# A hybrid decoder layer on one core: in the attention's blocks on TensorE the scores move ahead of the transposes, and two pairs' values move together

## The chip, the cores and the metric

The kernel runs on 1 core of one Trainium2 chip. The metric is device time in microseconds (us), the median of several runs. One further execution was taken by the hardware profiler; all rows of the trace are of that one.

Engines: PE is TensorE (matmuls), PEld its weight loads, DVE is VectorE, ACT is ScalarE, POOL is GpSimd, SP issues the DMAs.

## The reference, cut to what matters

One decoder layer, 256 tokens, width 1024, 8 heads of 64. With 256 tokens there is one MoBA block of 256 keys, so the attention is causal within it.

```
h = rmsnorm(x, norm_mix_g)
q, k, v, u_pool, gate_logits = split(h @ w_in)
q = rotary(rmsnorm(q, q_norm_g)); k = rotary(rmsnorm(k, k_norm_g))
attn = softmax(causal(q @ k.T * 64**-0.5)) @ v
pooled = multiscale_pool_mixer(u_pool, w_pool, pool_scale)
gates = sigmoid(gate_logits + b_gate)
x = x + (gates[0] * (attn @ w_branch_attn) + gates[1] * (pooled @ w_branch_pool)) @ w_out
h2 = rmsnorm(x, norm_ffn_g)
gate, val = split(causal_depthwise_conv(h2 @ w_up, conv_w, conv_b))
out = x + (silu(gate) * val) @ w_down
```

## The kernel before, in words

**Weights.** Each weight arrives by DMA as chunks of 128 x 2048 float32 (`raw`) and is split into a high part (`hi`, ACT, line 87) and a low part (`lo`, DVE, line 91), both of type float32r. A product is then three matmuls: high by high, low by high, high by low (`mm3`, lines 99 to 101). `ahead()` records the next splits between the matmuls of the current work, and a freed `raw` buffer starts the next load.

**Stages.** q, k and v (line 298), the pool inputs `u`, sixteen gate tiles `g0` to `g15` (24 matmuls each, `feature_tile`), eight tiles of the pool branch `bp` (12 matmuls each, `branch`), eight of the attention branch `ba`, the output projection, and the FFN (`up`, `down`), which fills the second half of the time.

**The attention** is put between the gate tiles and the pool branch's tiles, by pairs of heads `hp` = 0 to 3, in plain float32. For each pair there are three pieces on PE:

- `scores(hp)`: q by k, 4 matmul calls (lines 473, 474). Both heads have a contraction of 64, so one stands on rows 0 to 63 of the array and the other on rows 64 to 127 (the trace prints the array's part as 64\*128). Then DVE adds the mask and takes the maxima, ACT takes the exponentials, POOL multiplies by the reciprocal sums.
- `weigh(hp)`: six transposes of the probabilities, 128x128 each (line 506, tile `ps_p`, whole array, 128\*128); ACT copies the result to `pT` (line 508).
- `values(hp)`: v by `pT`, 4 matmul calls (line 517, tile `ps_o`). The two heads write 64 partitions each, so the trace prints 128\*64. ACT and DVE then make `ath` and `atl`, which the attention branch reads.

A matmul call in float32 is two instructions in the trace, a transpose is one; so the scores and the values have 8 each, the transposes 6.

**The order.** All is recorded in program order and every engine runs its own instructions in that order. `later(n, fn)` files a piece for n ticks later; `tick()` comes after every gate tile, and in the pool branch after the odd tiles. `scores` stands ahead of g1, g5, g9 and g13; `weigh` is filed 4 ticks after its scores, so it comes just after g4, g8, g12 and after `bp1`; `values` another 4 ticks later (after g8, g12, bp1), for the last pair 1 tick (after `bp3`). So between two gate tiles there stand together: after g4 the transposes of pair 0 and the scores of pair 1; after g8 the values of pair 0, the transposes of pair 1, the scores of pair 2; after g12 the same one pair on; after bp1 the values of pair 2 and the transposes of pair 3; after bp3 the values of pair 3.

**PSUM.** Pool `ps2` has two buffers of two banks each (scores, transposes and the pool maps `ps_m` use it in turn), pool `mm` four of one bank (all tiles, and the values).

Of the kernel before, what the change touches and what calls it, by code (L numbers as in the profile page):

```python
# [8 lines left out]
F32 = mybir.dt.float32  # L9
# [5 lines left out]
P = 128  # L15
# [7 lines left out]
KA = AW // P  # L23
# [43 lines left out]
def hybrid_layer_kernel(ctx: ExitStack, tc: tile.TileContext, xq_d, xtok_d, par_d, wkv_d, wpg_d,  # L67
# [11 lines left out]
    ps2 = pairs.enter_context(tc.tile_pool(name="ps2", bufs=2, space=bass.MemoryType.PSUM))  # L79
    tmp = mixer.enter_context(tc.tile_pool(name="tmp", bufs=2))  # L80

    def bank(name):
        return mm.tile([P, 512], F32, tag="mm", name=name)


    def high(hi, src, scale=1.0):
        nc.scalar.activation(hi, src, AF.Copy, scale=scale)  # L87

    def low(lo, hi, src, scale=None):
        if scale is None:  # L90
            nc.vector.tensor_tensor(lo, src, hi.bitcast(F32), ALU.subtract)  # L91
        else:
            nc.vector.scalar_tensor_tensor(lo, src, scale, hi.bitcast(F32), ALU.mult, ALU.subtract)
# [59 lines left out]
    def next_high():  # L153
        if at[0] < len(pieces):
            c, sl, first, _ = pieces[at[0]]
            if c - oldest() >= WBUFS:
                return
            at[0] += 1
            if first:
                moving = order[c][0] in "qkv"  # L160
                place = MOVING if moving else 0
                his[c] = whi_p.tile([P, CH + P], F32R, tag="whi", name=f"hi_{order[c][0]}{c}")[:, place:]
                place = MOVING if moving else FAR
                los[c] = wlo_p.tile([P, CH + P], F32R, tag="wlo", name=f"lo_{order[c][0]}{c}")[:, place:]
            high(his[c][:, sl], raw(c, sl))

    def next_low(eager=False):
        if at[1] < at[0] - STAGGER or at[0] == len(pieces) > at[1] or (at[1] < at[0] and eager):
            c, sl, _, last = pieces[at[1]]
            at[1] += 1  # L170
            low(los[c][:, sl], his[c][:, sl], raw(c, sl))
            if last:
                split.add(c)
                while loaded[0] - RAWBUFS in split and order[loaded[0] - RAWBUFS][0] != "q" and loaded[0] < len(order):
                    load()
# [221 lines left out]
    def later(n, fn, *args):  # L397
        due.setdefault(clock[0] + n, []).append((fn, args))
# [67 lines left out]

    TOK = (slice(0, P), slice(P, 3 * P))

    def scores(hp):
        ps = ps2.tile([P, 2, 512], F32, tag="ps2", name=f"ps_s{hp}")  # L470
        for j in range(2):
            rows = slice(j * DH, (j + 1) * DH)
            nc.tensor.matmul(ps[:, j, P:3 * P], qT[rows, hp, P:S], kT[rows, hp, :], start=True, stop=True)
            nc.tensor.matmul(ps[:, j, 0:P], qT[rows, hp, 0:P], kT[rows, hp, 0:P], start=True, stop=True)
        if hp == 0:

            for _ in range(2):
                next_high()
        sm = tmp.tile([P, 2, 3 * P], F32, tag="big", bufs=4, name=f"sm{hp}")
        nc.vector.tensor_tensor(sm, ps[:, :, 0:3 * P],  # L480
                                mask.rearrange("p a b -> p (a b)")[:, None, :].to_broadcast([P, 2, 3 * P]), ALU.add)
        mx = tmp.tile([P, 2, 2], F32, tag="mx", name=f"mx{hp}")
        for t in (1, 0):
            nc.vector.tensor_reduce(mx[:, t, :], sm[:, :, TOK[t]], axis=AX.X, op=ALU.max)
        nc.vector.scalar_tensor_tensor(mx, mx, -1.0, qs[:, :, 2 * hp:2 * hp + 2], ALU.mult, ALU.mult)
        if hp == 0:
            for _ in range(2):
                next_low()
        sums = tmp.tile([P, 2, 2], F32, tag="sums", name=f"sums{hp}")
        for j in range(2):  # L490
            for t in (1, 0):
                nc.scalar.activation(sm[:, j, TOK[t]], sm[:, j, TOK[t]], AF.Exp, bias=mx[:, t, j:j + 1],
                                     scale=qs[:, t, 2 * hp + j:2 * hp + j + 1], accum_out=sums[:, t, j:j + 1])
        rs = tmp.tile([P, 2, 2], F32, tag="rs", name=f"rs{hp}")
        nc.vector.reciprocal(rs, sums)
        for t in (1, 0):
            n = TOK[t].stop - TOK[t].start
            nc.gpsimd.tensor_tensor(sm[:, :, TOK[t]], sm[:, :, TOK[t]],
                                    rs[:, t, :, None].to_broadcast([P, 2, n]), ALU.mult)
        later(4, weigh, hp, sm)  # L500

    def weigh(hp, sm):
        pp = ps2.tile([P, 2, 512], F32, tag="ps2", name=f"ps_p{hp}")
        for j in range(2):
            for b in range(3):
                nc.tensor.transpose(pp[:, j, b * P:(b + 1) * P], sm[:, j, b * P:(b + 1) * P], ident)
        pT = tmp.tile([P, 2, 3 * P], F32, tag="big", bufs=4, name=f"pT{hp}")
        nc.scalar.activation(pT, pp[:, :, 0:3 * P], AF.Copy)
        later(1 if hp == KA - 1 else 4, values, hp, pT)

    def values(hp, pT):

        po = bank(f"ps_o{hp}")
        for b in range(2):
            for j in range(2):
                h = 2 * hp + j
                nc.tensor.matmul(po[j * DH:(j + 1) * DH, b * P:S], vn[:, b, h * DH:(h + 1) * DH],
                                 pT[:, j, 2 * b * P:(2 * b + 2 - b) * P], start=b == 0, stop=b == 1)
        high(ath[:, hp, :], po[:, 0:S])
        low(atl[:, hp, :], ath[:, hp, :], po[:, 0:S])  # L520
# [26 lines left out]
    for n in range(2 * KD):  # L547
        if n >= FIRST and (n - FIRST) % 4 == 0:
            scores((n - FIRST) // 4)
        if n == 10:  # L550
            pool_maps()
            ahead()
        b, c = n // 2, n % 2
        if c == 0:
            w = chunk("g")
        ps = feature_tile(w, c, f"g{n}")
        tick()
        ahead(AHEAD if n % 2 else 0)
        nc.vector.tensor_tensor(gate(n), ps[:, 0:S], R1, ALU.mult)
        if n >= 2 * KD - 2:  # L560
            sigmoids(3)
# [213 lines left out]
    last = {}  # L775
# [71 lines left out]
```

## Time and profile before

| what | value |
|---|---|
| median of 3 runs | 335.42 us (335.11 to 335.70) |
| the profiled execution's own time | 335.33 us |
| its span, first to last instruction | 333.6 us |
| PE busy / weight loads busy | 328.6 us (99%) / 319.5 us (96%) |
| DVE / ACT / POOL busy | 254.9 (76%) / 202.6 (61%) / 82.3 us (25%) |
| granted TensorE clock, mean | 0.998 |

The span lies 1.73 us below the execution's own time. "Busy" of PE counts an instruction from its start to its modelled end, so two matmuls that overlap in the pipeline look like one, and a matmul that waits for its weights inside its own row still looks busy. What PE loses is better seen in the time from one matmul to the next.

### The profile page before, as it was taken

What the parts mean: (1) busy time and instruction counts of PE and PEld (TensorE: products, weight loads), DVE (VectorE), ACT (ScalarE), POOL (GpSimd) and SP (SyncE); (2) the same over time, 40 slices, a digit from 0 to 9 for tenths busy, and PEclk for the clock granted to TensorE, in tenths of its full rate; (3) what the DMA queues carried; (4) which work ended last, traced back from release to release, by engine and by line L of the source; (5) the groups of instructions that cost most, each with busy time, mean ns of one, the idle gap of its engine ahead of it and who ended that gap; (6) DMA issues with size and microseconds to landing.
All of it is one profiled execution on the core that took longest, in us unless ns stands there. A gap on an engine that the chain in (4) does not pass through costs nothing.

```text
span 333.6 us, 6696 instructions
## 1 busy us (share of the span) xinstructions
PE 328.6 (99%) x2728; PEld 319.5 (96%) x2728; DVE 254.9 (76%) x408; ACT 202.6 (61%) x326; POOL 82.3 (25%) x98
## 2 busy tenths in 40 slices
PE   8999999999999999999999999999999999999995
PEld 7888899999999999999999999999999999999995
DVE  4939979979778866877997977777777777768844
ACT  5767626645849945767766766555656464646520
POOL 1007771102404034121241212121212121221330
PEclk9999999999999999999999999999999999999999
DMA  7999763474455660763529283636454555543003
GB/s 266 422 415 205 226 271 129 157 253 149 145 210 181 218 235 2 252 210 110 209 106 358 72 328 129 252 130 252 140 240 146 233 163 216 182 198 128 0 2 126
DMA packets 11102, 63.94 MB, mean 192 GB/s; under 512 B 1472, under 2 KB 2752, under 8 KB 4032
## 3 DMA queue, kind: packets, MB, share of 16 engines
q1 hardware_dynamic: 10656, 63.39, 53.3%
q8 instruction: 21, 0.34, 0.4%
q10 hardware_dynamic: 416, 0.13, 0.3%
q14 instruction: 9, 0.07, 0.1%
HBM read 62.47 MB, written 1.05 MB: 190 GB/s over the span
## 4 chain that ended last, share of the span: by engine, by line
PE 97%; DMA 1%; ACT 0%; DVE 0%; issue 0%
PE ps_up L99 12%; PE ps_up L101 12%; PE ps_up L100 12%; PE ps_d L707 6%; PE ps_d L709 6%; PE ps_d L708 6%; PE ps_g L99 5%; PE ps_g L101 4%; PE ps_g L100 4%; PE ps_q L298 3%; PE ps_k L298 3%; PE ps_v L298 3%; PE ps_out L99 2%; PE ps_out L101 2%; PE ps_out L100 2%; DMA xq<-in_xq 1%
## 5 line engine op out<-in xcount | busy, mean ns | idle before, releaser
L101 PE MATMUL ps_up<-hhi,lo_up 128*128 128x256 f32 x352 | 97.2, 276 | 0.0
L99 PE MATMUL ps_up<-hhi,hi_up 128*128 128x256 f32 x352 | 97.2, 276 | 0.0
L100 PE MATMUL ps_up<-hlo,hi_up 128*128 128x256 f32 x352 | 97.2, 276 | 0.0
L100 PEld LDWEIGHTS ps_up<-hlo,hi_up 128*128 128x128 f32 x352 | 66.1, 188 | 0.0
L101 PEld LDWEIGHTS ps_up<-hhi,lo_up 128*128 128x128 f32 x352 | 66.1, 188 | 0.0
L99 PEld LDWEIGHTS ps_up<-hhi,hi_up 128*128 128x128 f32 x352 | 66.1, 188 | 0.0
L91 DVE TENSOR_TENSOR lo_up<-raw_up,hi_up 128x1024 fp32r<-128x1024 f32 x44 | 54.7, 1261 | 7.3 <-ACT hi_up L87 7.3
L707 PE MATMUL ps_d<-ah,hi_dn 128*128 128x256 f32 x176 | 48.6, 276 | 0.0
L708 PE MATMUL ps_d<-al,hi_dn 128*128 128x256 f32 x176 | 48.6, 276 | 0.0
L709 PE MATMUL ps_d<-ah,lo_dn 128*128 128x256 f32 x176 | 48.6, 276 | 0.0
L689 POOL TENSOR_TENSOR c_v<-c_g,c_v 128x256 f32<-128x256 f32 x22 | 16.2, 736 | 121.4 <-DVE c_v L672 121.4
L87 ACT ACTIVATE hi_up<-raw_up 128x1024 fp32r<-128x1024 f32 x44 | 44.1, 1047 | 0.0
L87 ACT ACTIVATE ah<-c_v 128x256 fp32r<-128x256 f32 x22 | 9.2, 418 | 45.6 <-POOL c_v L689 45.6
L99 PE MATMUL ps_g<-xhi,hi_g 128*128 128x256 f32 x128 | 35.9, 280 | 0.0
L100 PE MATMUL ps_g<-xlo,hi_g 128*128 128x256 f32 x128 | 35.3, 276 | 0.0
L101 PE MATMUL ps_g<-xhi,lo_g 128*128 128x256 f32 x128 | 35.3, 276 | 0.0
L707 PEld LDWEIGHTS ps_d<-ah,hi_dn 128*128 128x128 f32 x176 | 33.0, 188 | 0.0
L708 PEld LDWEIGHTS ps_d<-al,hi_dn 128*128 128x128 f32 x176 | 33.0, 188 | 0.0
L709 PEld LDWEIGHTS ps_d<-ah,lo_dn 128*128 128x128 f32 x176 | 33.0, 188 | 0.0
L91 DVE TENSOR_TENSOR lo_dn<-raw_dn,hi_dn 128x1024 fp32r<-128x1024 f32 x22 | 27.8, 1263 | 0.4 <-ACT hi_dn L87 0.4
L677 DVE TENSOR_TENSOR u_v<-ps_up,R 128x256 f32<-128x256 f32 x22 | 9.3, 421 | 20.9 <-PE ps_up L101 20.8
L714 POOL TENSOR_TENSOR al<-c_v,ah 128x256 fp32r<-128x256 f32 x22 | 22.0, 1002 | 11.6 <-ACT ah L87 11.6
(188 smaller groups left out, 794.7 us busy)
## 6 DMA issues: line engine op xcount, KB each, us to landing
raw_up<-in_wup SPq DMA_DIRECT2D x22, 1024.0 KB, 4.9
raw_dn<-in_wdn SPq DMA_DIRECT2D x11, 1024.0 KB, 4.9
raw_g<-in_wpg SPq DMA_DIRECT2D x8, 1024.0 KB, 5.9
raw_o<-in_wout SPq DMA_DIRECT2D x4, 1024.0 KB, 4.7
raw_v<-in_wkv SPq DMA_DIRECT2D x2, 1024.0 KB, 15.4
raw_p<-in_wpg SPq DMA_DIRECT2D x2, 1024.0 KB, 12.9
raw_bp<-in_wbp SPq DMA_DIRECT2D x2, 1024.0 KB, 4.8
raw_ba<-in_wba SPq DMA_DIRECT2D x2, 1024.0 KB, 4.7
```

The costliest lines, as they stand in the source:

```text
L87: nc.scalar.activation(hi, src, AF.Copy, scale=scale)
L91: nc.vector.tensor_tensor(lo, src, hi.bitcast(F32), ALU.subtract)
L99: nc.tensor.matmul(out, sh, mh, start=start, stop=False, **kw)
L100: nc.tensor.matmul(out, sh, ml, start=False, stop=False, **kw)
L101: nc.tensor.matmul(out, sl, mh, start=False, stop=stop, **kw)
L298: nc.tensor.matmul(pt[t], sx[:, k, t * P:(t + 1) * P], wx[:, sl], start=k == 0 and sx is xhi and wx is hi, stop=k == KD - 1 and wx is lo)
L677: nc.vector.tensor_tensor(u, ps[:, 0:S], R2, ALU.mult)
L689: nc.gpsimd.tensor_tensor(uc[1], g[1], uc[1], ALU.mult)
L707: nc.tensor.matmul(o, hi[:, sl], acch[i], start=first, stop=False, skip_group_check=True)
L708: nc.tensor.matmul(o, hi[:, sl], accl[i], start=False, stop=False, skip_group_check=True)
L709: nc.tensor.matmul(o, lo[:, sl], acch[i], start=False, stop=i == KF - 1, skip_group_check=True)
L714: nc.gpsimd.tensor_tensor(accl[i], act_i, acch[i].bitcast(F32), ALU.subtract)
```

## The change

`weigh` of pairs 0 to 2 no longer runs at its tick. It is put on a list (`held`), and the next `scores` runs it right after its own matmuls. `weigh` of pair 3 runs at its tick as before. `values` of pair 2 is filed 5 ticks after its `weigh` in place of 4, which is the tick of pair 3's values; these two write the two banks of one `ps2` buffer (`ps_oo`) in place of two `mm` buffers.

```
+    held = []
+
     def scores(hp):
         ps = ps2.tile([P, 2, 512], F32, tag="ps2", name=f"ps_s{hp}")
         for j in range(2):
             rows = slice(j * DH, (j + 1) * DH)
             nc.tensor.matmul(ps[:, j, P:3 * P], qT[rows, hp, P:S], kT[rows, hp, :], start=True, stop=True)
             nc.tensor.matmul(ps[:, j, 0:P], qT[rows, hp, 0:P], kT[rows, hp, 0:P], start=True, stop=True)
+
+        while held:
+            weigh(*held.pop())
...
-        later(4, weigh, hp, sm)
+        later(4, weigh if hp == KA - 1 else lambda *a: held.append(a), hp, sm)
...
-        later(1 if hp == KA - 1 else 4, values, hp, pT)
+
+        later((4, 4, 5, 1)[hp], values, hp, pT)
+
+    last = []
 
     def values(hp, pT):
 
-        po = bank(f"ps_o{hp}")
+        if hp < KA - 2:
+            po = bank(f"ps_o{hp}")
+        elif hp == KA - 2:
+            last.append(ps2.tile([P, 2, 512], F32, tag="ps2", name="ps_oo"))
+            po = last[0][:, 0, :]
+        else:
+            po = last[0][:, 1, :]
```

How the order on the engines changes, at three places (names as built, with buffer numbers; the shapes are the outputs').

PE between gate tiles g12 and g13: values of pair 1 (`ps_o`), transposes of pair 2 (`ps_p`), scores of pair 3 (`ps_s`). Before:

```order
L517 MATMUL ps_o_1145<-pT_976,vn 64x256 x2
L517 MATMUL ps_o_1145<-pT_976,vn 64x128 x2
L506 MATMUL ps_p_1152<-ident,sm_990 128x128 x6
L473 MATMUL ps_s_1164<-qkT 128x256
L474 MATMUL ps_s_1164<-qkT 128x128
L473 MATMUL ps_s_1164<-qkT 128x256
L474 MATMUL ps_s_1164<-qkT 128x128
```

The same place now:

```order
L531 MATMUL ps_o_1145<-pT_988,vn 64x256 x2
L531 MATMUL ps_o_1145<-pT_988,vn 64x128 x2
L475 MATMUL ps_s_1155<-qkT 128x256
L476 MATMUL ps_s_1155<-qkT 128x128
L475 MATMUL ps_s_1155<-qkT 128x256
L476 MATMUL ps_s_1155<-qkT 128x128
L511 MATMUL ps_p_1160<-ident,sm_990 128x128 x6
```

The transposes moved from between values and scores to behind the scores, next to g13. The place after g8 reads the same; after g4 there are no values, and transposes and scores change places.

PE in the pool branch, after bp1 and after bp3 (the 12 matmuls of each `bp` tile are left out here). Now, behind bp1 and then behind bp3:

```order
L511 MATMUL ps_p_1312<-ident,sm_1169 128x128 x6
L531 MATMUL ps_oo<-pT_1167,vn 64x256 x2
L531 MATMUL ps_oo<-pT_1167,vn 64x128 x2
L531 MATMUL ps_oo<-pT_1319,vn 64x256 x2
L531 MATMUL ps_oo<-pT_1319,vn 64x128 x2
```

The first row stands alone behind bp1, where the values of pair 2 stood ahead of it; the other four stand behind bp3, where the values of pair 3 stood alone.

ACT over the same two tiles (`pT`: the copy of the transposes of pair 3; `ath`: the high part of the values; `hi_ba`: a weight split; the `xq` rows are sigmoids). Before:

```order
L527 ACTIVATE xq<-xq,par 128x256
L87 ACTIVATE ath<-ps_o_1312 128x256
L508 ACTIVATE pT_1326<-ps_p_1319 128x768
L87 ACTIVATE hi_ba_1328<-raw_ba_1117 128x1024
L527 ACTIVATE xq<-xq,par 128x256
L87 ACTIVATE hi_ba_1328<-raw_ba_1117 128x1024
L527 ACTIVATE xq<-xq,par 128x256
L87 ACTIVATE ath<-ps_o_1366 128x256
```

Now:

```order
L541 ACTIVATE xq<-xq,par 128x256
L513 ACTIVATE pT_1319<-ps_p_1312 128x768
L87 ACTIVATE hi_ba_1321<-raw_ba_1117 128x1024
L541 ACTIVATE xq<-xq,par 128x256
L87 ACTIVATE hi_ba_1321<-raw_ba_1117 128x1024
L541 ACTIVATE xq<-xq,par 128x256
L87 ACTIVATE ath<-ps_oo 128x256 x2
```

The `ath` of pair 2 left its place ahead of the copy and stands beside that of pair 3. On DVE its low part moved likewise; nothing else changes there. In the gate tiles the copy `pT` moves behind one weight split on ACT, still ahead of the exponentials.

## Rows read from the trace of the kernel before

**Rows 1.** The page's busy line, and the waits of PE (us in total, times, longest).

```profile
PE 328.6 (99%) x2728; PEld 319.5 (96%) x2728; DVE 254.9 (76%) x408; ACT 202.6 (61%) x326; POOL 82.3 (25%) x98
...
PE ps_warm L228 <- DVE ones L196: 1.1, 1, 1.1
PE ps_q L298 <- ACT hi_q L87: 0.4, 1, 0.4
```

**Rows 2.** Windows: stretch, length, busy PE PEld DVE ACT POOL, PEclk, DMA, GB/s.

```profile
78.09:80.99 2.90, 2.90 (x27) 2.14 (x26) 2.39 (x4) 1.36 (x3) 0.00 (x0) 1.00 0.89 302
...
110.89:112.11 1.22, 1.22 (x12) 0.78 (x11) 1.22 (x2) 1.22 (x3) 0.00 (x0) 1.00 0.41 54
112.11:117.45 5.34, 5.34 (x48) 5.34 (x48) 4.46 (x9) 4.99 (x11) 0.00 (x0) 1.00 0.77 267
```

**Rows 3.** Chain that ended last, between g0 and g1: start us, us, what.

```profile
53.80 0.64 PE ps_s L473 x4
54.44 0.22 PE ps_s L474 x4
54.66 0.31 PE ps_g L99
```

**Rows 4.** The same chain between g4 and g5.

```profile
65.74 0.66 PE ps_p L506 x6
66.39 0.64 PE ps_s L473 x4
67.03 0.22 PE ps_s L474 x4
67.25 0.32 PE ps_g L99
```

**Rows 5.** The same chain between g8 and g9.

```profile
78.37 0.80 PE ps_o L517 x8
79.17 0.81 PE ps_p L506 x6
79.97 0.64 PE ps_s L473 x4
80.61 0.22 PE ps_s L474 x4
80.84 0.31 PE ps_g L99
```

**Rows 6.** The same chain between g12 and g13, first and last piece.

```profile
93.28 0.80 PE ps_o L517 x8
...
95.74 0.31 PE ps_g L99
```

**Rows 7.** The same chain behind bp1.

```profile
106.82 0.80 PE ps_o L517 x8
107.62 0.81 PE ps_p L506 x6
108.43 0.12 PE ps_bp L99
```

**Rows 8.** The same chain behind bp3.

```profile
111.16 0.80 PE ps_o L517 x8
111.96 0.32 PE ps_bp L99
```

**Rows 9.** Timeline of PEld at g0's end and g4's end: start, us, instruction.

```profile
53.72 0.31 PEld L473 LDWEIGHTS ps_s<-qkT 64*128 64x128 f32 x4
...
65.48 0.67 PEld L506 LDWEIGHTS ps_p<-ident,sm 128*128 128x128 f32 x6
```

**Rows 10.** Timelines of DVE, PE and ACT at the buffers that change hands.

```profile
81.44 0.95 DVE L480 TENSOR_TENSOR sm<-ps_s,mask 128x768 f32<-128x768 f32 x1
...
83.59 0.28 PE L99 MATMUL ps_m<-poolh,hi_pool 128*128 128x256 f32 x1
...
109.06 0.79 ACT L508 ACTIVATE pT<-ps_p 128x768 f32<-128x768 f32 x1
```

## Prediction

> **What bounds the kernel now.** I read the busy line and the waits first. PE is busy 328.6 of 333.6 us, and its waits for other engines are two at the very start, 1.1 and 0.4 us [rows 1]. So from the first projection on nothing holds PE back but PE: every engine behind it has room, and the time is the sum of what stands on PE. Next I read the windows, to see whether the attention's pieces cost clock: across the whole block after g8 the granted clock is 1.00, the 2.4 GHz level, and it is the same in the pool branch [rows 2]. A change in the order of PE's instructions can then act in two ways only: through what PE loses between its instructions, or through a new wait for another engine.
>
> What it loses is seen in the chain that ended last, which there is PE's own sequence. The reader should compare the length of one kind of piece after different neighbours. The six transposes take 0.66 us behind a gate tile [rows 4] and 0.81 us behind values [rows 5, 7]. The first matmul of a tile takes 0.31 or 0.32 us behind scores and behind values [rows 3, 4, 5, 8], but 0.12 us behind transposes [rows 7]. The scores take 0.64 + 0.22 = 0.86 us behind a gate tile and behind transposes alike [rows 3, 4, 5]. The values, always behind a tile, take 0.80 us [rows 5, 6, 7, 8]. So there is a charge at some borders and none at others. It is 0.81 - 0.66 = 0.15 us for entering transposes and 0.31 - 0.12 = 0.19 us (0.20 with 0.32) for entering a tile, and it falls where the part of the array changes: scores use 64\*128, tiles and transposes 128\*128 [rows 9], values 128\*64. Between tiles and transposes the part stays the same, and there is no charge in either direction. The weight loads show why: ahead of transposes the first load stands at 65.48, 0.26 us before the 65.74 at which the chain begins that piece, while ahead of scores it stands at 53.72, only 0.08 us before 53.80 [rows 3, 4, 9]. At a border of this kind the load isn't drawn ahead under the matmuls in front of it.
>
> The Trainium skill (TensorEngine Tiling (Array Packing), Key Properties) says that changing the tiling mode, not just the tile, drains TensorE. The charges above are that drain, at 0.15 to 0.20 us each; the page gives no price, and the sum below goes by the rows.
>
> **The change, part by part.** I call a border that changes the part a switch.
>
> *After g4.* Before: transposes 0.66, scores 0.86, first matmul of g5 0.32, which is 1.84 us [rows 4]. Now scores come behind a tile, 0.86 as after g0 [rows 3]; transposes come behind scores; the first matmul of g5 comes behind transposes, 0.12 [rows 7]. Transposes behind scores have no row. Behind a part that doesn't change they take 0.66, behind values 0.81. I take 0.81, since scores change the part as values do. Sum 1.79, so -0.05 us. Two switches stand there before and after; only their prices differ. With 0.66 it would be -0.20.
>
> *After g8 and g12.* Before: 0.80 + 0.81 + 0.86 + 0.31 = 2.78 us [rows 5], and the second place has the same length, 93.28 to 95.74 against 78.37 to 80.84 [rows 5, 6]. There are four switches: into values, into transposes, into scores, into the tile. Now it is values 0.80, scores behind values, transposes behind scores 0.81, tile 0.12: three switches. Scores behind values have no row either. From below they take 0.86 less a switch, some 0.67; from above the 0.86 that they take behind whatever the rows show. I take 0.86, as both their neighbours in the rows are a change of part and values to scores is one too (128\*64 to 64\*128). Sum 2.59, so -0.19 at each place, -0.38 for both.
>
> *Behind bp1.* Before: values 0.80, transposes 0.81, tile 0.12, which is 1.73 [rows 7]. Now the transposes alone, with tiles on both sides: 0.66 + 0.12 = 0.78 [rows 4, 7]. That is -0.95.
>
> *Behind bp3.* Before: 0.80 + 0.32 [rows 8]. Now two pairs' values in a row, and the second needs no switch. Values without a switch have no row: at most 0.80, and at least 0.80 less the dearest entry, 0.20, which is 0.60. I take 0.65, the 0.80 less the 0.15 that the transposes pay for entering behind values, the nearest row. That is +0.65, with ends at +0.60 and +0.80. Behind bp1 and bp3 together: -0.30, two switches fewer.
>
> *Other engines.* ACT, DVE and POOL do what they did, so nothing is removed there. ACT's copy `pT` moves behind one weight split in the gate tiles, and stays ahead of exponentials that can't start before DVE has the maxima; values need it only four ticks later. No DMA is added or moved in SP's queue.
>
> *Buffers.* The turn of the two `ps2` buffers changes. The pool maps, ahead of g10, now get the buffer of pair 2's scores, which is free when DVE has added the mask: 81.44 + 0.95 = 82.39. PE reaches the maps at 83.59, or 83.35 with the 0.24 us saved by then [rows 10]. That leaves 0.96 us, and before it was a transposes' copy long done, so no cost as long as DVE keeps its time. The values of pair 3 need the copy of pair 3's transposes, done at 109.06 + 0.79 = 109.85 before [rows 10]. ACT is full there (1.22 of 1.22 us behind bp3, 4.99 of the next 5.34 [rows 2]), so I let the copy gain only the `ath` row that leaves its front, and bound its end by 109.85 above and some 0.3 us less below, about 109.55. The values of pair 2 now begin 0.05 + 0.38 + 0.95 = 1.38 us earlier than 111.16, at 109.78, and those of pair 3 0.65 later, at 110.43. That leaves 0.6 to 0.9 us: again no wait. What both feed, the attention branch, starts at 117.45 [rows 2] behind four more tiles.
>
> **Sum.** -0.05 - 0.38 - 0.95 + 0.65 = -0.73 us. PE waits for nothing behind it, so all of it should reach the end. Against the profiled execution, 335.33 us, this gives 334.60; its span would be 332.9. That execution lies 0.09 below the median of the runs, 335.42, so the median should be **334.69 us**, 0.22% less. A measurement of this kernel can tell about 0.2%, 0.67 us, from no change; the forecast lies 0.06 us beyond that bound, so its own chances are split there.
>
> **The rivals.**
>
> *1. Scores behind values are free, and transposes behind scores too.* If the charge hung on the kind of work and not on the part (float32 pieces with half-array shapes as one kind), values to scores would cost nothing: another 0.19 at each of two places, -1.11 in all, 334.3 us; with transposes at 0.66 too, 0.15 more at each of three places. For it: no row shows the two side by side. Against it: every row where the part changes shows a charge. The page's rule on tiling modes speaks against it too, since 128 by 64 and 64 by 128 are different modes there. Chance 0.10.
>
> *2. Part of it is given back in small change.* The first matmuls behind a switch sometimes follow each other at 0.12 in place of 0.11 us; the second pair's values may pay the whole 0.80. With that 0.15 and some 0.15 of such small change the sum is -0.43, 334.99 us, which counts as the same. Chance 0.14.
>
> *3. A new wait behind bp3, slower than before.* ACT is full there and PE now arrives 1.38 us earlier, with 0.6 to 0.9 us to spare for the copy of pair 3's transposes. From the point at which that copy comes more than 0.9 us late PE waits, and what stands behind on PE waits with it. It eats the whole gain when the copy is 0.9 + 0.73 = 1.63 us late, and makes the kernel slower by more than 0.67 from 2.3 us on, two weight splits or three. With 2.4 us it gives 335.42 - 0.73 + 1.5 = 336.2 us. For it: ACT's full windows. Against it: the order puts no split ahead of the copy that wasn't there before, and one `ath` fewer. Chance 0.04.
>
> *4. The change does nothing that counts.* The charges in the chain would be an artefact of where the profile puts a matmul's end, and the order of pieces would be free: 335.4 us. Against it: the same pieces agree at all places to 0.01 us, and the windows in front and behind add up. Chance 0.05.
>
> **How the numbers follow.** The forecast has 0.67; measured with some 0.25 us of spread (the three runs lie within 0.6 us), 0.06 us beyond the bound, it gives 0.38 faster and 0.29 same. Rival 1 gives 0.10 faster, rivals 2 and 4 0.19 same, rival 3 0.04 slower. Together 0.48 faster, 0.48 same, 0.04 slower. The range reaches from rival 1, 334.3 less 0.1 of spread, up to rival 2 with its spread, 335.2: **334.2 to 335.2 us**.
>
> **What the profile after would show.** Right: in the chain after g8 and g12 values 0.80, scores 0.86, transposes 0.81, tile 0.12; behind bp1 transposes 0.66; behind bp3 sixteen instructions of values in about 1.45 us, then a tile's first matmul at 0.32; PE's waits still only those at the start; a span near 332.9 us. Scores behind values shorter than 0.75 us would show rival 1. A wait of PE for ACT's `pT` in the pool branch would show rival 3, and one for DVE's `sm` ahead of the pool maps its like. The forecast is wrong if the pieces shorten as said and the span doesn't: then something behind, DVE or a weight's arrival, was closer to PE than its missing waits tell.

## The result and the profile after

The change made the kernel slower: 338.62 us (median of six runs, 337.34 to 338.82) against 335.34 us before (335.11 to 335.70), a ratio of 1.0088 (95% interval 1.0070 to 1.0106). The forecast was 334.69 us with a range up to 335.2. The profiled execution took 338.81 us, 3.48 more than that of before, on a span of 337.0 us.

First the line and the view with which the prediction began: the page's busy line of the changed kernel, and the waits of PE (total us, times, longest).

```profile
PE 329.9 (98%) x2728; PEld 320.9 (95%) x2728; DVE 255.6 (76%) x408; ACT 202.8 (60%) x326; POOL 82.4 (24%) x98
...
PE ps_oo L531 <- DVE atl L91: 2.2, 1, 2.2
PE ps_warm L228 <- DVE ones L196: 1.1, 1, 1.1
PE ps_q L298 <- ACT hi_q L87: 0.3, 1, 0.3
```

Against [rows 1] there is one wait more, and it is the only one past the first microseconds: PE waited 2.2 us for DVE's `atl` before it could write `ps_oo`, the buffer that the values of pairs 2 and 3 share. Now the windows (columns as in [rows 2]), from the end of bp3 to the start of the attention branch:

```profile
109.69:113.80 4.11, 1.92 (x19) 1.05 (x18) 2.29 (x4) 2.76 (x5) 0.00 (x0) 0.98 0.76 267
113.80:117.14 3.34, 3.34 (x18) 3.34 (x16) 2.26 (x5) 3.23 (x6) 0.00 (x0) 0.51 0.01 5
117.14:120.92 3.78, 3.78 (x35) 3.78 (x34) 2.04 (x4) 1.44 (x4) 0.00 (x0) 1.00 0.80 284
```

In the first stretch PE is busy 1.92 of 4.11 us; in the second it is never idle, but the granted clock is 0.51, so nearly all of the stretch is at the lower of the two levels (1.2 GHz), where before the clock was 1.00 throughout [rows 2]. So the loss has two parts in a row: a pause, and a stretch at half clock behind it. The timelines of PE, ACT and DVE there:

```profile
109.90 0.87 PE L531 MATMUL ps_oo<-pT,vn 128*64 128x256 f32 x8
112.96 0.91 PE L531 MATMUL ps_oo<-pT,vn 128*64 128x256 f32 x8 [2.19 <-DVE atl L91]
113.80 0.58 PE L99 MATMUL ps_bp<-poolh,hi_bp 128*128 128x256 f32 x1
114.18 0.42 PE L100 MATMUL ps_bp<-pooll,hi_bp 128*128 128x256 f32 x1
```

```profile
108.70 0.80 ACT L513 ACTIVATE pT<-ps_p 128x768 f32<-128x768 f32 x1
109.40 1.04 ACT L87 ACTIVATE hi_ba<-raw_ba 128x1024 fp32r<-128x1024 f32 x1
110.34 0.50 ACT L541 ACTIVATE xq<-xq,par 128x256 f32<-128x256 f32 x1
110.74 1.04 ACT L87 ACTIVATE hi_ba<-raw_ba 128x1024 fp32r<-128x1024 f32 x1
111.69 0.50 ACT L541 ACTIVATE xq<-xq,par 128x256 f32<-128x256 f32 x1
112.09 0.36 ACT L87 ACTIVATE ath<-ps_oo 128x256 fp32r<-128x256 f32 x1
```

```profile
112.48 0.42 DVE L91 TENSOR_TENSOR atl<-ps_oo,ath 128x256 fp32r<-128x256 f32 x1 [0.45 <-ACT ath L87]
```

Read from the bottom up, pair 3's values start at 112.96, when DVE has finished `atl` of pair 2 (112.48 + 0.42 = 112.90). DVE had waited for `ath`, and ACT came to `ath` at 112.09, because two weight splits and two sigmoids stand between `pT` and it. When pair 2's values ended, at 110.77, ACT still had one of each to go through. Pair 3's own input, `pT`, was done at 109.50. In the program the readers of pair 2's half are written ahead of pair 3's matmuls, and the two halves are one tile; so the write of the second half waits for the readers of the first, though they touch other banks.

The moves themselves did what was forecast. The chain around the place after g8:

```profile
78.45 0.80 PE ps_o L531 x8
79.25 0.64 PE ps_s L475 x4
79.89 0.22 PE ps_s L476 x4
80.11 0.81 PE ps_p L511 x6
80.92 0.12 PE ps_g L99
```

Against [rows 5] the values take 0.80 and the scores behind them 0.86, the transposes 0.81, the tile's first matmul 0.12 in place of 0.31: so there is one switch less, as written in the sum.

### The profile page after: what moved, and what is told of

It reads as the page before. It is cut to its first block, busy times and chain, and to the rows that moved or that the text cites. A ratio compares the mean times of both kernels' runs of the same rounds, so it can differ in the third digit from the quotient of the medians.

```text
span 337.0 us, 6695 instructions
## 1 busy us (share of the span) xinstructions
PE 329.9 (98%) x2728; PEld 320.9 (95%) x2728; DVE 255.6 (76%) x408; ACT 202.8 (60%) x326; POOL 82.4 (24%) x98
## 4 chain that ended last, share of the span: by engine, by line
PE 92%; ACT 4%; DVE 1%; DMA 1%; issue 1%; ACTq 0%
PE ps_up L101 12%; PE ps_up L100 12%; PE ps_up L99 12%; PE ps_d L723 6%; PE ps_d L722 6%; PE ps_d L721 6%; PE ps_g L99 4%; PE ps_g L101 4%; PE ps_g L100 3%; PE ps_q L298 3%; PE ps_k L298 3%; PE ps_v L298 3%; PE ps_out L101 2%; PE ps_out L100 2%; PE ps_out L99 2%; ACT hi_ba L87 1%
```

## The experiments

**A buffer for each pair (own_buffers).** The change, with the shared tile parted:

```
-        elif hp == KA - 2:
-            last.append(ps2.tile([P, 2, 512], F32, tag="ps2", name="ps_oo"))
-            po = last[0][:, 0, :]
         else:
-            po = last[0][:, 1, :]
+            po = ps2.tile([P, 2, 512], F32, tag="ps2", name=f"ps_oo{hp}")[:, 0, :]
```

> The change, but the values of pair 2 and of pair 3 each in a ps2 buffer of their own in place of the two halves of one. Wait theory (pair 3's values waited because they share a buffer with pair 2's, whose readers on ACT and DVE stand ahead of them in the program; that pause also halved the clock for 3.4 us): no wait of PE for DVE behind bp3, clock 1.00 there, sixteen instructions of values in about 1.45 us, 0.73 us under the kernel before, 334.6 us. Late-copy theory (ACT is full and the copy pT of pair 3 comes late, whatever the buffer): the pause stays at about 2.2 us, now put down to ACT, and the time stays at 337 to 339 us.

Measured: 334.61 us (334.47 to 334.65), ratio to the kernel before 0.9975 (0.9965 to 0.9985). PE has no wait past the start. The chain behind bp3, and the window from the tile bp4 to the attention branch:

```profile
109.72 1.45 PE ps_oo L528 x16
111.17 0.32 PE ps_bp L99
```

```profile
111.10:116.67 5.57, 5.57 (x51) 5.57 (x50) 5.03 (x10) 5.57 (x12) 0.00 (x0) 1.00 0.65 215
```

The sixteen instructions of values take 1.45 us, the forecast's 0.80 + 0.65, and the clock stays at 1.00. The late-copy theory, which is the prediction's third rival, falls: ACT is as full here (5.57 of 5.57 us), and nothing waits for its copy. The run also gives both prices of the change. From the start of pair 2's values to that of bp4 the change takes 113.80 - 109.90 = 3.90 us, against 1.45 here: the pause costs 2.45. From bp4 to the attention branch the change takes 3.34 + 3.78 = 7.12 us, against 5.57 here: the half clock costs 1.55. Together that is 4.00, and the two medians are 4.01 apart. The two profiled executions, from which these prices are taken, are 4.29 apart; another 0.25 stood there long before the attention, where the first matmul of k starts at 16.61 in the change and at 16.36 here. That is a difference of executions and not of the programs.

**The shared buffer, with its readers behind (readers_behind).** The buffer of the change stays; only the order of the program differs (the list `last` now holds the pairs whose values are still to be read):

```
...
-        high(ath[:, hp, :], po[:, 0:S])
-        low(atl[:, hp, :], ath[:, hp, :], po[:, 0:S])
+        last.append((hp, po))
+        if hp == KA - 2:
+            return
+        for f, o in ((h, o) for h, o in last[-2:] if hp == KA - 1 or h == hp):
+            high(ath[:, f, :], o[:, 0:S])
+            low(atl[:, f, :], ath[:, f, :], o[:, 0:S])
```

> The change with its one shared buffer, but ACT's and DVE's reading of pair 2's values is written behind pair 3's matmuls. Wait theory: the wait hangs on the order in the program, not on the buffer, so it goes here too: 334.6 us, and the values of pair 3 wait at most for ACT's copy, under 0.1 us. If the sharing of the buffer itself cost time (both halves written while one is read): 335 us or more, with the charge in the rows of pair 3's values. Late-copy theory: 337 to 339 us.

Measured: 334.57 us (334.43 to 335.24), ratio 0.9980 (0.9971 to 0.9988), no wait of PE past the start. Its values of both pairs take the same 1.45 us:

```profile
109.61 1.45 PE ps_oo L532 x16
111.06 0.32 PE ps_bp L99
```

So the buffer itself costs nothing that these runs show. What cost was that a reader of one half stood in the program ahead of the writer of the other.

**The scores alone (scores_only).** Pairs 2 and 3 as in the kernel before:

```
-        later((4, 4, 5, 1)[hp], values, hp, pT)
+        later((4, 4, 4, 1)[hp], values, hp, pT)
...
+        po = bank(f"ps_o{hp}")
```

> Only the scores ahead of the transposes; the values as in the kernel before. Wait theory: -0.05 after g4 and -0.19 each after g8 and g12, -0.43 in all, 334.9 us, no new wait. If the order of the pieces were free (my rival 4): 335.3 us.

Measured: 334.84 us (334.68 to 335.55), ratio 0.9981 (0.9972 to 0.9990), where the before of the same session has 335.36. That is -0.52 by the medians against -0.43 forecast, and the chains show the same pieces as in the change. The rival by which the order of the pieces is free falls.

**The values alone (values_only).** The transposes go back to their tick, ahead of the scores:

```
-        while held:
-            weigh(*held.pop())
...
-        later(4, weigh if hp == KA - 1 else lambda *a: held.append(a), hp, sm)
+        later(4, weigh, hp, sm)
```

> Only the second part of the change: pair 2's values with pair 3's in one shared ps2 buffer; the transposes ahead of the scores as in the kernel before. Wait theory: two switches fewer (-0.30), and the whole pause behind bp3 as in the change, 2.2 us of PE waiting for DVE, with the clock falling in most runs: 0.43 above the change, about 339.0 us (337.7 where the clock stays). If the loss came of the moved transposes: 335.0 us.

Measured: 338.71 us (four runs, 337.75 to 338.93), ratio 1.0091 (1.0075 to 1.0107). The loss is here, so it comes of the second part. But I expected 0.43 more than the change, and it is only 0.09 more. The timeline shows why:

```profile
109.91 0.87 PE L529 MATMUL ps_oo<-pT,vn 128*64 128x256 f32 x8
112.78 0.89 PE L529 MATMUL ps_oo<-pT,vn 128*64 128x256 f32 x8 [2.00 <-DVE atl L91]
```

Pair 3's values start at 112.78 here and at 112.96 in the change, though the change saves 0.43 us ahead of them. Two things lie in this difference. The executions were apart before anything that was changed: the first matmul of k starts at 16.21 here and at 16.61 in the change. And the end of the pause is set by ACT's queue, which by the rows hangs on the values of pair 1, the first piece behind g12, by way of their `ath` and DVE's `atl`. Here and then in the change they stand at:

```profile
92.93 0.87 PE L529 MATMUL ps_o<-pT,vn 128*64 128x256 f32 x8
```

```profile
93.10 0.87 PE L531 MATMUL ps_o<-pT,vn 128*64 128x256 f32 x8
```

From there to ACT's next exponentials it is 5.43 us here and 5.44 in the change (they start at 98.36 and 98.54; in the kernel before it is 5.43 too), and to pair 3's values 19.85 and 19.86. So what PE saves behind pair 1's values, the 0.19 after g12, only makes the pause longer, 2.19 in place of 2.00 us. What it saves ahead of them, the 0.05 after g4 and the 0.19 after g8, is kept: from the first matmul of k to pair 1's values it is 76.72 us here and 76.49 in the change. My expectation missed that and should have been 0.24 above the change, not 0.43. The medians can't show 0.24: they come from different sessions, and against the kernel before of its own session this run is 3.24 us slower, the change 3.28.

**The pause filled (filled_wait and filled_part).** The change, with matmuls that nothing reads put between the two pairs' values, 20 in the one and 6 in the other:

```
+        if hp == KA - 1:
+            fill = ps2.tile([P, 2, 512], F32, tag="ps2", name="ps_fill")
+            for _ in range(20):
+                nc.tensor.matmul(fill[:, 0, 0:S], ones_r, xhi[:, 0, :], start=True, stop=True)
```

> The change, with 20 matmuls of 128x256 float32r into an unread buffer between the values of pair 2 and of pair 3, about 2.3 us of work where PE waits. Wait theory, with the clock falling on account of the pause: pair 3's values start when they do in the change (112.9 us), the clock stays at 1.00, and the 1.7 us that the rows at half clock cost come back: 337.1 us in every run. If the clock falls for another reason (the half-array pieces in a row): 338.6 us as in the change.

> As the run with 20 matmuls in the pause, but with 6, which leave PE waiting for about 1.3 us. Pair 3's values still wait for DVE until about 112.9 us. If a shorter pause doesn't lower the clock: 1.00 throughout and 337.0 us. If any pause of over 1 us here does: 338.6 us, with a stretch at 0.50 behind it.

Measured with 20: 337.52 us (337.25 to 337.72). The wait is gone and the clock stays at 1.00, as the window of the stretch that was at half clock in the change shows:

```profile
113.80:117.14 3.34, 3.34 (x32) 3.10 (x29) 2.34 (x5) 2.76 (x5) 0.00 (x0) 1.00 0.07 25
```

It is 0.4 us over the expectation. Most of that is the filling itself, which with the two switches around it takes longer than the pause:

```profile
110.88 2.65 PE L531 MATMUL ps_fill<-xhi,ones_r 128*128 128x256 f32 x20
113.47 0.87 PE L535 MATMUL ps_oo<-pT,vn 128*64 128x256 f32 x8
```

Counted from pair 1's values, at 93.29 in this execution, pair 3's values start after 20.18 us, 0.32 later than in the change.

Measured with 6: 337.03 us (336.89 to 337.70), as expected for a clock that stays. Its timeline and the same window:

```profile
111.08 0.97 PE L531 MATMUL ps_fill<-xhi,ones_r 128*128 128x256 f32 x6
113.33 0.87 PE L535 MATMUL ps_oo<-pT,vn 128*64 128x256 f32 x8 [1.28 <-DVE atl L91]
```

```profile
113.80:117.14 3.34, 3.34 (x32) 3.15 (x29) 2.47 (x5) 2.89 (x5) 0.00 (x0) 1.00 0.11 44
```

PE did idle 1.28 us, and kept its clock. So in the traces of these runs the clock fell behind bp3 only after the whole pause, of 2.0 to 2.2 us. The pieces on half of the array, two pairs' values in a row, don't bring it down: the run with own buffers has them too, at 1.00. The run with 6 differs from the change in two things at once, a shorter pause and 0.97 us of work ahead of it, and doesn't tell which of them kept the clock.

**The values in the tiles' banks (banks).** Same places, but both pairs' values in one-bank buffers of the tiles:

```
-        if hp < KA - 2:
-            po = bank(f"ps_o{hp}")
...
+        po = bank(f"ps_o{hp}")
```

> The change with the two pairs' values at the same place, but in two of the four one-bank buffers of the tiles, as the values stood before. Wait theory: no wait for pair 2's readers, but the tile bp4 now needs the bank of bp2, which DVE empties at 111.8 in the run with own buffers, where bp4 starts at 111.1: a wait of about 0.7 us, and some 0.1 more at bp5; 335.4 us, no gain. If four banks are enough: 334.6 us.

Measured: 335.50 us (335.10 to 336.04), ratio 1.0003 (0.9994 to 1.0013), the expected loss of the whole gain. The timeline shows the wait where it was expected, at bp4, for DVE to empty a bank:

```profile
109.68 1.52 PE L525 MATMUL ps_o<-pT,vn 128*64 128x256 f32 x16
111.86 0.38 PE L99 MATMUL ps_bp<-poolh,hi_bp 128*128 128x256 f32 x1 [0.66 <-DVE xq L590]
```

The pairs' buffers are thus the right place for these values; one buffer for both, with readers in between, was not.

**One block of values less (pairs01).** On top of own buffers, the values of pair 0 wait for those of pair 1:

```
-        later((4, 4, 5, 1)[hp], values, hp, pT)
+        later((8, 4, 5, 1)[hp], values, hp, pT)
```

> The version with own buffers, and the values of pair 0 moved behind g12 too, to stand with pair 1's (each in its own bank). One block of values and its two switches less: behind g8 0.80 goes, behind g12 0.65 comes, -0.15: 334.45 us. If pair 1's values wait for a bank or for readers, as pair 3's did in the change, PE shows a wait behind g12 and the time rises above 334.6 us.

Measured: 334.45 us (334.29 to 334.67), ratio 0.9968 (0.9957 to 0.9980), no wait of PE past the start. Behind g12:

```profile
92.42 1.45 PE ps_o L528 x16
93.87 0.64 PE ps_s L475 x4
94.51 0.22 PE ps_s L476 x4
94.73 0.81 PE ps_p L511 x6
```

It has the lowest median of all versions, 0.16 below own buffers as the sum of its rows says. That step is inside the two intervals, and the two were measured in different sessions; so that it beats own buffers rests on the rows, and that it beats the kernel before is measured.

## Why the prediction was wrong

*What bounds the kernel* was right: PE alone, with no wait behind the start. That is also why a single new wait shows in full.

*The switches* were right in price and number. After g8 and g12 three remain in place of four; scores behind values pay the full 0.86, and transposes behind scores 0.81, the two prices that had no row. Rival 1, by which they are free, falls. The second pair's values cost 0.65, as taken. The Trainium skill (TensorEngine Tiling (Array Packing), Key Properties) says that changing the tiling mode drains TensorE. The traces agree: scores take as long behind values, 0.86 us, as behind a tile. Without the wait the forecast of 334.69 us is met by two versions, 334.61 and 334.57.

*Buffers* is the step that failed: "That leaves 0.6 to 0.9 us: again no wait." I asked there only when pair 3's input `pT` would be ready, and it was, at 109.50. (The 0.6 to 0.9 has a slip: pair 2's values in front take 0.80 us and not 0.65, so pair 3's would have begun at 110.58, with 0.7 to 1.0 us left. The conclusion on `pT` is the same.) I didn't ask who must be done with the buffer that pair 3 writes. Its other half had just been filled by pair 2, and pair 2's readers, `ath` on ACT and `atl` on DVE, stand in the program between the two writes. In the rows of the order both `ath` stood side by side ahead of the prediction, which looked harmless; for ACT's own order it was. With that dependency in view, the rows shown would have pointed at the pause: ACT full behind bp3 [rows 2] meant a late `ath`; DVE follows, and then PE. It measured 2.19 us, where the sum had no term at all. The half clock behind it, 1.55 us, stood in no row of the kernel before.

*Sum*: "PE waits for nothing behind it, so all of it should reach the end" fell with it. Of the -0.73 us, the 0.24 saved after g4 and g8 was kept; the rest lies behind pair 1's values and went into the pause. From the start of those values to that of bp4 it is 18.69 us before, 18.25 with own buffers and 20.70 in the change. The pause and the clock brought 4.00 us on top of the version without a wait.

*Rival 3* named the place, the full ACT, and the sign, but the wrong releaser: the copy `pT` of pair 3, where it was `ath` and `atl` of pair 2. Its price per microsecond was also too low: it had no half clock behind the wait. Its chance of 0.04 was that of a copy running late; a wait for a reader that stands in line on a full engine needed no lateness at all.

## What to carry to other kernels

When two results are put into one buffer, list the readers of the first that the program writes ahead of the writer of the second: here the second waited for them, though it touches another bank. Write the readers behind both, or give each its own buffer. Time such a wait by the queue of the engine that reads, not by its work: here `ath` takes 0.36 us, and started 1.3 us after pair 2's values had ended, behind a weight split and a sigmoid.

## What the runs showed of the hardware

A pause of 2.19 us on PE, which past the start waits for nothing else here, was followed by 3.34 us at a granted clock of 0.51, and these cost 1.55 us more. It was not so in every execution. Of the six of the change four had a mean clock of 0.993 to 0.995 and took 338.59 to 338.82 us, and two had 0.998 and took 337.34 and 337.69; of the four with the values alone, one had 1.000 and took 337.75. That is most of the spread of these runs. The four and the two lie 1.2 us apart on average, less than the 1.55 of the profiled execution; the others left no trace, so what the two lost is not known. Behind a pause of 1.28 us none of five executions had a mean clock below 0.999. Why the clock falls in one execution and not in another is not settled by these runs.

A switch of the array's part costs 0.15 us here into transposes and into values (the 0.80 of the first pair against the 0.65 of the second), and 0.19 or 0.20 into a tile. Into scores the price isn't known, since no run has scores without a switch. Transposes next to tiles are no switch in either direction (0.66 and 0.12 us). The order of small pieces on PE could thus be counted by its borders.
